# The last half of the output projections: tokens as the outer loop, weight blocks as the inner one

## The chip, the cores and the metric

The kernel runs on one core of a Trainium2 chip. The metric is the device time of one execution in microseconds (us). The core has engines with an instruction queue each: TensorE (PE, matmuls), VectorE (DVE), ScalarE (ACT), GpSimd (POOL), and SyncE (SP), which issues the DMA transfers. They meet only through semaphores.

## The reference

Two layers work on 512 tokens of width 1024. Each adds a gated mixer and a gated mixture of experts to the residual h. This is the part that matters here, cut:

```
for layer in range(2):
    mod = silu(c) @ w_ada[layer] + b_ada[layer]
    sh1, sc1, gt1, sh2, sc2, gt2 = split(mod, 6)
    u = rms_norm(h, norm1) * (1 + sc1) + sh1
    m = mixer_ab(u, ...) if layer == 0 else mixer_c(u, ...)     # both end with  y @ w_out
    h = h + gt1 * m
    u = rms_norm(h, norm2) * (1 + sc2) + sh2
    h = h + gt2 * hier_moe(u, w_grp, b_grp, w_rt, b_rt, w1, w3, w2)
return rms_norm(h, final_norm)
```

`hier_moe` computes 36 logits for each token (4 groups and 32 experts), picks the best group and the two best experts in it, and runs every token through those two (32 experts of 1024 x 512, 512 x 1024 in all).

## The kernel before, in words

All tokens stand on the chip as four tiles t = 0 to 3 of 128 tokens (NT = 4). The program goes through startup, mixer of layer 0, experts of layer 0, mixer of layer 1, experts of layer 1. The weights are streamed from HBM.

**The output projection.** `out_steps` makes `h += gt1 * (y @ w_out)`. It goes over two halves hb = 0, 1 of the 1024 output columns, and over K blocks of 128 rows of `w_out`. A block's half, 128 x 512, is multiplied by the gate (VectorE or GpSimd in turn), and then split (`split`): ScalarE copies it to a rounded part `whi` (L395), and GpSimd subtracts that from it, which gives `wlo` (L396). Both lie in the pool `whl`, which has three buffers of each. `mm3` then makes three matmuls for a tile of tokens: `yhi x whi` (L402), `yhi x wlo` (L403), `ylo x whi` (L404). `steps_rows` makes one step of each block k: its preparation does the gate and the split, and its matmuls go over the four tiles of tokens, so four PSUM banks are open at a time, and all four sums become complete in the last step, three matmuls apart.

When the sum of a tile is complete, `use(t, p)` adds it to h on VectorE (L502). In the last `out_steps` of a layer (K = 4 in layer 0, with `yB`; K = 2 in layer 1, with `yc`) it also calls `done(t, hb)`: that spawns the logits of this half tile, and ScalarE squares the half row of h and sums it (L1309). The logits are four transposes of h on TensorE (L516), a copy to SBUF on VectorE (L1319) or ScalarE (L1321), and, one tick of the stream later, matmuls with the router's weights (L1326). A tick is one `yield` of a step, that is, six matmuls. At the end of all tiles stand the sum of the squares (L1311), a square root on ScalarE (L1312), the reciprocal r (L1313), and on VectorE the logits `lg` from PSUM (L1332), times r (L1333), plus the bias (L1334).

**From there to the experts.** VectorE picks groups and experts in some 25 small instructions, which end with `selb` (L1628). TensorE counts the chosen tokens (L1633, L1634, L1658), VectorE makes places of them (`posm`, L1635) and from those the matrices `Dm` that gather tokens (L1411), TensorE gathers with them (L1426), and the experts' first matmuls (L1502) follow. Meanwhile ScalarE and GpSimd make the normalised h in two parts, `hhi` (L1338) and, for three of the tiles' first halves, `hlo` (L1341, L1342 on GpSimd); VectorE makes the rest (L1347). Two groups of dummy matmuls (`warm`, L178, 20 and 10) stand in TensorE's queue before and after the counting.

**What sets the order.** `run_steps` prepares steps up to two ahead of the one whose matmuls are issued. The order of instructions on each engine is fixed when the program is built: a planner simulates the engines and the pools' buffers, so that a pool with another number of buffers can change the order of all that uses it. The pools `whl` serve all projections of the layer, not only the last.

Of the kernel before, what the change touches and what calls it, by code (L numbers as in the profile page):

```python
# [17 lines left out]
P = 128  # L18
# [3 lines left out]
NT = T // P  # L22
# [67 lines left out]
class Build:  # L90
# [386 lines left out]
    def loader(self, thunks):  # L477
# [3 lines left out]
        def ask(i):  # L481
            if i < len(thunks) and i not in tiles:
                tiles[i] = thunks[i]()
            return tiles.get(i)
# [5 lines left out]
        ask(0)  # L490
        ask(1)

    def out_steps(self, y, K, i0, gate, done=None):


        nc = self.nc
        out = []
        for hb in range(2):
            s = slice(hb * 512, hb * 512 + 512)

            def use(t, p, hb=hb, s=s):
                nc.vector.tensor_add(self.h(t)[:, s], self.h(t)[:, s], p)  # L502
                if done:
                    done(t, hb)

            def ws(k, hb=hb, s=s):
                i = i0 + k // 2
                return self.raw(i)[:, k % 2, s], lambda: self.raw_done(i) if hb and k % 2 else None
            out += self.steps_rows(y, K, ws, use, lambda s=s: gate()[:, s])
        return out  # L510

    def u_transposed(self, hn, h):
# [1269 lines left out]
    def build(self):  # L1782
        tc, nc, a = self.tc, self.nc, self.a
        self.n_ext = 7
        right_side = dict(side="right")
        self.mod, self.ready = {}, set()
        with ExitStack() as es0:
            self.const = self.pool(es0, "const")
            self.gates = self.pool(es0, "gates", 1)
            self.small = self.pool(es0, "small", 2)  # L1790
            self.ring = self.pool(es0, "ring", 2)
            self.psum = self.pool(es0, "psum", 8, space=PSUM)
            self.hroom = self.pool(es0, "hroom", 2)
            self.uroom = self.pool(es0, "uroom", 4)
            self.new_h()
            for l in range(2):
                with ExitStack() as es:
                    self.mix = self.pool(es, "mix%d" % l, 2, **right_side)
                    self.whl = self.pool(es, "whl%d" % l, 3, **right_side)
                    right = self.pool(es, "right%d" % l, 1, **right_side)  # L1800
                    self.stream = st = Stream()
                    with ExitStack() as ms:
                        ut = [self.uroom.tile([P, 4, T], F32R, name="w", tag="w") for _ in range(4)]
                        u = lambda i, k, ut=ut: ut[2 * i + k // 4][:, k % 4]
                        vp = self.pool(ms, "v%d" % l, 2 - l)
                        us = ExitStack()
                        tmp = self.pool(us, "ut%d" % l, 1, **right_side)
                        if l == 0:
                            fin = self.mixer_ab(u, ms, right, *self.startup(u, tmp, us, vp))
                        else:  # L1810
                            fin = self.mixer_c(u, ms, right, self.restart(u, tmp, us, vp))
                        st.until(lambda: not st.q)
                    os_ = ExitStack()
                    self.moe_open(l, os_)
                    self.run_steps(st, fin)
                    st.until(lambda: not st.q)
                self.dump_h("hm%d" % l)
                self.moe(os_)
                if l:
                    self.finish()  # L1820
                os_.close()
                self.dump_h("ho%d" % l)
# [137 lines left out]
```

## Time and profile before

| what | value |
|---|---|
| median of 3 runs | 1747.19 us (1747.1 to 1747.67) |
| the profiled execution's own time | 1746.73 us |
| its span, first to last instruction | 1745.0 us |
| mean granted TensorE clock | 0.973 |
| TensorE busy | 1651.2 us, 95% of the span |
| VectorE, ScalarE, GpSimd busy | 46%, 30%, 23% |
| DMA, mean | 284 GB/s |

How to read it: the profiled execution lies 0.46 us below the median, and 1.73 us of it lie outside the span. TensorE is busy in nearly all of the span; VectorE in less than half of it. The busy shares are means over stages that differ. Times in the rows below are us from the span's start.

### The profile page before, as it was taken

The numbers are of one execution on the slowest core, as the hardware profiler recorded it, in microseconds if no ns is written. First come the engines' busy times: TensorE is split into PE (matmuls) and PEld (weight loads), VectorE is DVE, ScalarE is ACT, GpSimd is POOL, SyncE is SP. The second block draws the span as 40 slices with busy tenths as digits, with TensorE's granted clock in tenths as the row PEclk, the third lists the DMA queues.
The fourth block names the chain that finished last, engine by engine and source line by source line (L and its number), as shares of the span: only waits on it lengthen the run. The fifth ranks groups of instructions, "written<-read, shape, count | busy, mean of one in ns | idle before, by whom it ended". The sixth has DMA issues, their size and how long they took to land. (4 is left out here: it accounts for less than half of the span.)

```text
span 1745.0 us, 23263 instructions
## 1 busy us (share of the span) xinstructions
PE 1651.2 (95%) x9036; PEld 1003.2 (57%) x9036; DVE 806.4 (46%) x1793; ACT 518.9 (30%) x1027; POOL 394.8 (23%) x350
## 2 busy tenths in 40 slices
PE   6999999899999999998988989899999999999996
PEld 3666767544554555454667667678544554555453
DVE  2344653532433233335687787865432433243324
ACT  4745332310110111014636475364310110111013
POOL 2443523210010101001534343353210010101011
PEclk9999999999999999998999999999999999999998
DMA  8655655589999999994243432237599999999992
GB/s 300 223 173 175 217 185 216 221 358 380 413 413 412 413 411 414 411 409 137 63 141 111 132 110 85 85 106 281 226 368 378 413 411 412 413 411 414 412 407 106
DMA packets 156051, 495.89 MB, mean 284 GB/s; under 512 B 16216, under 2 KB 43156, under 8 KB 140576
## 3 DMA queue, kind: packets, MB, share of 16 engines
q1 hardware_dynamic: 155488, 493.23, 73.4%
q8 instruction: 74, 1.21, 0.3%
q10 hardware_dynamic: 448, 1.11, 0.2%
q14 instruction: 41, 0.34, 0.1%
HBM read 492.21 MB, written 2.10 MB: 283 GB/s over the span
## 5 line engine op out<-in xcount | busy, mean ns | idle before, releaser
L1502 PE MATMUL ps<-w,XTm 128*64 128x512 f32 x2048 | 447.2, 593 | 0.0
L1502 PEld LDWEIGHTS ps<-w,XTm 128*64 128x64 f32 x2048 | 161.7, 137 | 267.6 <-issue 260.7
L396 POOL TENSOR_TENSOR wlo<-w,whi 128x512 fp32r<-128x512 f32 x136 | 181.5, 1339 | 269.1 <-ACT whi L395 251.4
L1556 PE MATMUL ps<-w,hT 128*64 128x512 f32 (+1 forms) x1056 | 230.9, 587 | 1.0 <-ACT hT L1534 1.0
L1525 DVE TENSOR_TENSOR gg<-gg,ps 128x512 f32<-128x512 f32 x32 | 22.0, 688 | 377.4 <-PE ps L1502 377.3
L402 PE MATMUL ps<-w,whi 128*128 128x512 f32 x384 | 165.6, 432 | 0.0
L403 PE MATMUL ps<-w,whi 128*128 128x512 f32 x384 | 155.2, 405 | 2.1 <-POOL w L526 1.5
L1556 PEld LDWEIGHTS ps<-w,hT 128*64 128x64 f32 x1056 | 82.2, 137 | 130.2 <-issue 117.5
L404 PE MATMUL ps<-w,wlo 128*128 128x512 f32 x384 | 155.4, 405 | 0.0
L1579 DVE TENSOR_TENSOR w<-w,ps 128x512 f32<-128x512 f32 (+1 forms) x248 | 149.4, 665 | 7.0 <-PE ps L1570 5.5
L1511 POOL CAST sel<-ident 32x128 fp32r<-32x128 f32 x32 | 9.0, 280 | 591.7 <-PE ps L1539 533.9
L1560 POOL TENSOR_TENSOR yl<-y,yh 128x512 fp32r<-128x512 f32 x60 | 76.4, 1274 | 251.3 <-ACT yh L1559 251.3
L1559 ACT ACTIVATE yh<-y 128x512 fp32r<-128x512 f32 (+1 forms) x66 | 40.8, 618 | 295.4 <-DVE y L1558 294.4
L395 ACT ACTIVATE whi<-w 128x512 fp32r<-128x512 f32 x136 | 84.4, 627 | 147.5 <-PE ps L403 81.0
L1426 PE MATMUL ps<-Dm,hhi 128*128 128x256 f32 x512 | 126.2, 288 | 0.0
L1426 PE MATMUL ps<-Dm,hlo 128*128 128x256 f32 x512 | 123.6, 284 | 0.0
L1558 DVE SCALAR_TENSOR_TENSOR y<-ps,wsl,gate 128x512 f32<-128x512 f32 (+1 forms) x66 | 48.5, 735 | 151.5 <-issue 76.3
L1426 PEld LDWEIGHTS ps<-Dm,hhi 128*128 128x128 f32 x512 | 101.5, 199 | 13.4 <-issue 13.3
L1570 PE MATMUL ps<-yh,dt 128*128 128x512 f32 (+1 forms) x264 | 106.0, 406 | 0.0
L1534 ACT ACTIVATE hT<-ps 128x512 f32<-128x512 f32 x32 | 19.1, 598 | 284.2 <-PE ps L1532 265.9
L1426 PEld LDWEIGHTS ps<-Dm,hlo 128*128 128x128 f32 x512 | 101.6, 199 | 0.1
L1570 PE MATMUL ps<-yl,dt 128*128 128x512 f32 (+1 forms) x264 | 100.9, 387 | 0.0
(520 smaller groups left out, 2433.4 us busy)
## 6 DMA issues: line engine op xcount, KB each, us to landing
w<-in_moe_w_dram SPq DMA_DIRECT2D x380, 1024.0 KB, 14.9
w<-in_w_ada_dram SPq DMA_DIRECT2D x40, 1024.0 KB, 5.5
w<-in_w_in_c_dram SPq DMA_DIRECT2D x16, 1024.0 KB, 9.0
w<-in_w_in_ab_dram SPq DMA_DIRECT2D x10, 1024.0 KB
wst<-in_w_ada_dram SPq DMA_DIRECT2D x8, 1024.0 KB, 12.9
w<-in_w_out_ab_dram SPq DMA_DIRECT2D x4, 1024.0 KB, 4.8
w<-in_moe_w_dram SPq DMA_DIRECT2D x8, 512.0 KB, 15.2
w<-in_w_out_c_dram SPq DMA_DIRECT2D x4, 1024.0 KB, 4.9
```

Source lines behind the costliest of these rows:

```text
L395: nc.scalar.activation(hi, src, AF.Copy)
L396: nc.gpsimd.tensor_sub(lo, src, hi.bitcast(F32))
L402: mm(p, lhs[0], rhs[0], start=start, stop=False)
L403: mm(p, lhs[0], rhs[1], start=False, stop=False)
L404: mm(p, lhs[1], rhs[0], start=False, stop=stop)
L1426: nc.tensor.matmul(p, spread(src[:, t], k // 4)[k % 4], Dm[:, t].rearrange("p e s -> p (e s)"), start=t + i == 0, stop=t == NT - 1 and i == 1)
L1502: self.nc.tensor.matmul(ps[j][half[e]], X[:, k, half[e]], w, start=k == 0, stop=k == KD - 1)
L1556: nc.tensor.matmul(py[half[e]], hT[:, k, half[e]], w, start=k == 0, stop=k == 3)
L1558: nc.vector.scalar_tensor_tensor(y32, py, wsl, gate[:, c], op0=OP.mult, op1=OP.mult)
L1560: (nc.vector if last else nc.gpsimd).tensor_sub(yl[:, c], y32, yh[:, c].bitcast(F32))
L1570: mm = nc.tensor.matmul(p, dt[:, t * P:(t + 1) * P], y[:, s], start=i == 0, stop=i == 1)
L1579: nc.vector.tensor_add(h, h, p)
```

## The change

A new `steps_tiles` takes the place of `steps_rows` for the second half (hb = 1) of the last `out_steps` of each layer. It has one step for each tile of tokens; in it, all K blocks of weights are multiplied into one PSUM bank, and `use` follows at once. The preparation of step t does the blocks 2t and 2t + 1, so all blocks stand ready after the second step's preparation, and they are kept until the last tile. For that `whl` gets a fourth buffer in layer 0, where K = 4; in layer 1 it stays at three. The number of instructions on each engine stays the same.

```diff
+    def steps_tiles(self, xs, K, ws, use, scale):
+
+        W = []
+
+        def step(t):
+            def prep():
+                for k in range(2 * t, min(2 * t + 2, K)):
+                    w, after = ws(k)
+                    (self.nc.vector if k % 2 else self.nc.gpsimd).tensor_mul(w, w, scale())
+                    W.append(self.split(w, [P, 512]))
+                    after()
+
+            def mm(_):
+                p = self.ps()
+                for k in range(K):
+                    self.mm3(p, xs(k, t), W[k], k == 0, k == K - 1)
+                    if k % 2:
+                        if k == K - 1:
+                            use(t, p)
+                        yield
+            return prep, mm
+        return [step(t) for t in range(NT)]
...
-            out += self.steps_rows(y, K, ws, use, lambda s=s: gate()[:, s])
+            steps = self.steps_tiles if done and hb else self.steps_rows
+            out += steps(y, K, ws, use, lambda s=s: gate()[:, s])
...
-                    self.whl = self.pool(es, "whl%d" % l, 3, **right_side)
+                    self.whl = self.pool(es, "whl%d" % l, 4 - l, **right_side)
```

In the changed kernel the lines behind the new function have numbers that are 24 higher (the transposes L516 are L540, the logits' matmuls L1326 are L1350).

Three places show what the order of instructions becomes.

TensorE, layer 0, second half, around the end of the first sums. Before, the last block of weights (`whi_2388`) meets the tiles of tokens in turn, and the transposes of the first two tiles (`ps_2426`, `ps_2432`) stand behind the matmuls of the later tiles:

```order
L402 MATMUL ps_2362<-whi_2388,yBhi_1770 128x512 [waits Activation_49]
L403 MATMUL ps_2362<-wlo_2389,yBhi_1770 128x512 [waits Pool_49]
L404 MATMUL ps_2362<-whi_2388,yBlo_1771 128x512
L402 MATMUL ps_2363<-whi_2388,yBhi_1921 128x512
L403 MATMUL ps_2363<-wlo_2389,yBhi_1921 128x512
L404 MATMUL ps_2363<-whi_2388,yBlo_1922 128x512
L402 MATMUL ps_2364<-whi_2388,yBhi_2076 128x512
L516 MATMUL ps_2426<-ident_107,w_76 128x128 [waits DVE_49]
L516 MATMUL ps_2426<-ident_107,w_76 128x128 x3
L403 MATMUL ps_2364<-wlo_2389,yBhi_2076 128x512
```

Now, the first tile's sum (`ps_2367`) ends with its own last block, and its transposes (`ps_2391`) stand directly behind that:

```order
L402 MATMUL ps_2367<-whi_2305,yBhi_1770 128x512
L403 MATMUL ps_2367<-wlo_2306,yBhi_1770 128x512 [waits Pool_49]
L404 MATMUL ps_2367<-whi_2305,yBlo_1771 128x512
L402 MATMUL ps_2367<-whi_2310,yBhi_1770 128x512
L403 MATMUL ps_2367<-wlo_2311,yBhi_1770 128x512 [waits Pool_49]
L404 MATMUL ps_2367<-whi_2310,yBlo_1771 128x512
L540 MATMUL ps_2391<-ident_107,w_76 128x128 [waits DVE_49]
L540 MATMUL ps_2391<-ident_107,w_76 128x128 x3
L402 MATMUL ps_2397<-whi_2283,yBhi_1921 128x512 [waits PE_49]
```

Four matmuls of other tiles stood between a tile's last matmul and its transposes; now there is none. The same holds for the second and the third tile, and the logits' matmuls of tiles 0 to 2 stand in the middle of the next tile's twelve matmuls, where before all four stood behind the last matmul.

TensorE, layer 1, second half, the same place (K = 2, so six matmuls make a tile). Now:

```order
L402 MATMUL ps_9988<-whi_9891,ychi_9519 128x512
L403 MATMUL ps_9988<-wlo_9892,ychi_9519 128x512
L404 MATMUL ps_9988<-whi_9891,yclo_9520 128x512
L1350 MATMUL ps_9997<-wr_6090,scratch_9853 128x36 [waits DVE_49]
L1350 MATMUL ps_9997<-wr_6090,scratch_9853 128x36 x3
L540 MATMUL ps_10002<-ident_107,w_2935 128x128 [waits DVE_49]
L540 MATMUL ps_10002<-ident_107,w_2935 128x128 x3
L402 MATMUL ps_10008<-whi_9886,ychi_9519 128x512 [waits PE_49]
```

Here the logits' matmuls of the tile before (L1350, four instructions that the profile counts as eight) stand between a tile's last matmul and its transposes.

GpSimd, at the startup. The first projection of layer 0 has its low parts of u (`w` from `uf`, L526, now L550) between the splits of the weights. Before:

```order
L396 TENSOR_TENSOR wlo_259<-w_146,whi_258 128x512
L526 TENSOR_TENSOR w_89<-uf_315,w_87 128x512
L396 TENSOR_TENSOR wlo_340<-w_146,whi_339 128x512
L526 TENSOR_TENSOR w_89<-uf_323,w_87 128x512
L396 TENSOR_TENSOR wlo_357<-w_146,whi_356 128x512
```

Now:

```order
L396 TENSOR_TENSOR wlo_259<-w_146,whi_258 128x512
L550 TENSOR_TENSOR w_89<-uf_315,w_87 128x512
L396 TENSOR_TENSOR wlo_340<-w_146,whi_339 128x512
L396 TENSOR_TENSOR wlo_357<-w_146,whi_356 128x512
L550 TENSOR_TENSOR w_89<-uf_323,w_87 128x512
```

With the fourth buffer the fourth split (`wlo_357`) is put ahead of the second low part of u (`w_89<-uf_323`).

## Rows read from the trace of the kernel before

**Rows 1.** Windows, the experts of layer 0: busy us of each engine, clock, DMA share, GB/s

```profile
600.00:620.00 20.00, 20.00 (x97) 10.46 (x93) 5.84 (x13) 2.45 (x4) 2.54 (x2) 1.00 1.02 411
```

**Rows 2.** Windows (PE, PEld, DVE, ACT, POOL, clock, DMA share, GB/s), layer 0's tail

```profile
297.00:308.00 11.00, 11.00 (x55) 9.16 (x55) 2.63 (x5) 2.53 (x6) 1.29 (x1) 1.00 0.28 98
...
323.60:328.40 4.80, 4.79 (x25) 2.22 (x25) 4.16 (x22) 0.00 (x0) 0.00 (x0) 0.50 0.00 0
```

**Rows 3.** Timeline of PE, layer 0: start, duration, what, xcount [idle before, releaser]

```profile
304.85 0.39 PE L404 MATMUL ps<-whi,yBlo 128*128 128x512 f32 x1
...
306.02 0.74 PE L516 MATMUL ps<-ident,w 128*128 128x128 f32 x4
306.52 0.49 PE L403 MATMUL ps<-wlo,yBhi 128*128 128x512 f32 x1
...
308.00 0.39 PE L404 MATMUL ps<-whi,yBlo 128*128 128x512 f32 x1
308.24 1.87 PE L1326 MATMUL ps<-wr,scratch 128*128 128x36 f32 x16
309.94 1.18 PE L516 MATMUL ps<-ident,w 128*128 128x128 f32 x8
...
323.61 0.19 PE L1634 MATMUL ps<-selb,trixb 128*128 128x32 bf16 x1 [4.48 <-DVE selb L1628]
...
332.63 7.09 PE L1502 MATMUL ps<-w,XTm 128*64 128x512 f32 x32
```

**Rows 4.** Timeline of DVE, layer 0

```profile
305.28 1.37 DVE L502 TENSOR_TENSOR w<-w,ps 128x512 f32<-128x512 f32 x2 [7.30 <-PE ps L404]
...
313.86 0.31 DVE L1333 TENSOR_TENSOR lg<-lg,r 128x144 f32<-128x144 f32 x1
...
315.74 1.30 DVE L1605 TENSOR_TENSOR go<-go,gf 128x16 f32<-128x16 f32 x1
...
323.33 0.23 DVE L1628 CAST selb<-self 128x128 bf16<-128x128 f32 x1
```

**Rows 5.** Timeline of ACT, layer 0

```profile
306.00 0.63 ACT L1309 ACTIVATE hhi<-w 128x512 fp32r<-128x512 f32 x1 [6.17 <-DVE w L502]
...
311.21 0.60 ACT L1321 ACTIVATE scratch<-ps 128x512 f32<-128x512 f32 x1 [1.34 <-PE ps L516]
311.83 1.28 ACT L1312 ACT_TABLE_LOAD   x1
```

**Rows 6.** Timeline of PE, layer 1

```profile
1223.38 0.39 PE L404 MATMUL ps<-whi,yclo 128*128 128x512 f32 x1
...
1237.60 0.18 PE L1634 MATMUL ps<-selb,trixb 128*128 128x32 bf16 x1 [3.09 <-DVE selb L1628]
...
1245.39 1.08 PE L1502 MATMUL ps<-w,XTm 128*64 128x512 f32 x4
```

**Rows 7.** Timeline of DVE, layer 1

```profile
1229.15 0.31 DVE L1333 TENSOR_TENSOR lg<-lg,r 128x144 f32<-128x144 f32 x1
...
1237.32 0.23 DVE L1628 CAST selb<-self 128x128 bf16<-128x128 f32 x1
```

**Rows 8.** Timeline of POOL, layer 0's tail

```profile
315.73 1.28 POOL L1342 TENSOR_TENSOR hlo<-hn,hhi 128x512 fp32r<-128x512 f32 x1
```

**Rows 9.** Timeline of POOL, the startup

```profile
34.90 1.26 POOL L526 TENSOR_TENSOR w<-uf,w 128x512 fp32r<-128x512 f32 x1
37.46 1.28 POOL L396 TENSOR_TENSOR wlo<-w,whi 128x512 fp32r<-128x512 f32 x1 [1.30 <-ACT whi L395]
```

**Rows 10.** Timeline of PE, the startup

```profile
36.21 0.50 PE L403 MATMUL ps<-w,whi 128*128 128x512 f32 x1 [1.25 <-POOL w L526]
```

**Rows 11.** Timeline of PE, layer 0's mixer

```profile
102.65 0.50 PE L403 MATMUL ps<-wlo,w 128*128 128x512 f32 x1 [0.50 <-POOL wlo L396]
...
108.94 1.87 PE L265 MATMUL ps<-fold,modrow 128*128 128x1 f32 x8 [3.15 <-DVE modrow L333]
```

**Rows 12.** Timeline of PE, layer 0's mixer, behind a wait of TensorE

```profile
278.80 0.63 PE L404 MATMUL ps<-whi,yBlo 128*128 128x512 f32 x1
```

## The prediction

> **What bounds the kernel now.** I read the summary first, then the windows of the expert stages, then the timelines of the stretches between them. In the experts TensorE is busy 20.00 of 20 us at full clock [rows 1], and it waits for no load there. So a microsecond won or lost ahead of the experts is not made up inside them: it goes through to the end. What counts is when the first expert matmul L1502 starts: 332.63 in layer 0 and 1245.39 in layer 1 [rows 3, 6].
>
> Ahead of it lie two kinds of stretch. In the second half of the last projection, 297 to 308, TensorE is busy 11.00 of 11 us at full clock [rows 2]; it is the bound. Behind its last matmul (308.00 in layer 0, 1223.38 in layer 1 [rows 3, 6]) the chain runs over other engines: add, transposes, copy, square root, then VectorE's routing, `lg` times r at 313.86 and `selb` at 323.33. TensorE then idles 4.48 us for `selb` [rows 3, 4]. In layer 1 the same chain is 1223.38, 1229.15, 1237.32, with 3.09 us of idle [rows 6, 7]. So the edit is judged by two questions: when does the last projection matmul start, and how long is the chain from there.
>
> **The change, layer 0.** Nothing is added or removed; matmuls, adds, squares and copies are as many as before. Two things move the last matmul.
>
> First, the work of the logits that stood behind it comes ahead of it. Sixteen logits matmuls (two tiles) take 308.24 to 309.94, 1.70 us, so 0.85 a tile; the transposes of a tile take 306.02 to 306.52, 0.50 [rows 3]. Tiles 0 and 1's logits matmuls (1.70), tile 2's transposes (0.50) and tile 2's logits matmuls (0.85) are now ahead: 3.05 us. TensorE has no idle time to hide them in [rows 2].
>
> Second, the cover of the adds goes. The way from a tile's last matmul to its transposes is: 304.85 to 305.28, 0.43 until the add starts [rows 3, 4]; one add, 0.69, half of the 1.37 for two [rows 4]; 0.05 until 306.02 [rows 3]. That is 1.17 us, and before it was filled by four matmuls of the next tiles. Now the transposes stand in TensorE's queue directly behind the tile's last matmul, so TensorE stands still for 1.17 less the 0.23 that a matmul takes anyway (308.00 to 308.24 is 0.24 [rows 3]): 0.94 us for each of tiles 0, 1, 2, in all 2.82. All twelve matmuls of the next tile are queued behind that wait. Bounds: 0 if the wait were hidden, 2.82 as worked out; I take the whole, since the same add and the same transposes were timed.
>
> The last matmul then starts at 308.00 + 3.05 + 2.82 = 313.87. What follows it is shorter, as only one tile is left. The add ends 1.12 after it (0.43 + 0.69); the transposes start at 1.17 and, 0.74 long, end at 1.91 [rows 3]. ScalarE has squared by then (0.63 [rows 5]) and copies: from the copy's start at 311.21 to the table load at 311.83 are 0.62, and from the table load to L1333 at 313.86 another 2.03 [rows 4, 5]. With 0.04 until the copy starts L1333 comes 1.95 + 0.62 + 2.03 = 4.60 after the last matmul, against 313.86 - 308.00 = 5.86 before. So it stands at 318.47, **4.6 us later**. The routing behind it keeps its order and its partners on GpSimd, which start with the same r. Bounds: without the stalls +1.8; with the stalls and no shorter chain +5.9.
>
> **Layer 1.** Ahead of the last matmul come 1.70 of logits matmuls and 0.50 of transposes. The logits matmuls of the tile before stand in the gap of the add, so 0.23 + 0.85 of 1.17 are covered, and 0.09 a tile is left, 0.3 in all. The last matmul starts at 1223.38 + 2.5 = 1225.9. There is no table load in this layer's chain, so the last to arrive is the logits' sum: copy done 2.57 behind the last matmul, eight logits matmuls (0.85, and 0.17 until the last result: sixteen are 1.87 long but 1.70 apart [rows 3]), and 0.34 for L1332: 3.9. That gives L1333 at 1229.8, **+0.6** on 1229.15 [rows 7].
>
> Two more terms belong here. The routing from L1333 to `selb` takes 9.47 us in layer 0 and 8.17 in layer 1 [rows 4, 7]. The difference is in VectorE instructions that meet one of GpSimd's L1342: an instruction on 128x16 takes 1.30 us at 315.74, beside an L1342 that starts at 315.73 [rows 4, 8]. The Trainium skill (SBUF — State Buffer, section "Who interferes with whom") says that a VectorE instruction with two SBUF inputs contends with a GpSimd instruction that reads SBUF, and that the loser blocks fully; by that rule the size of the loss depends on the phase alone, and the trace agrees (1.30 us here). In layer 1, r and with it GpSimd move later against the routing, towards the phase of layer 0; I take half of the difference, **+0.65** (bounds 0 and 1.3). From `selb` to L1502 are 9.30 us in layer 0 and 8.07 in layer 1 [rows 3, 4, 6, 7]. In layer 1 three small instructions of the weights stood ahead of `posm`, and in the new order `posm` is first, as in layer 0; the first expert matmuls then wait for the same chain, and TensorE's idle time ahead of it grows from 3.09 towards layer 0's 4.48, after which the dummy matmuls ran at half clock (0.50 [rows 2]). I take layer 0's 9.30, **+1.2** (bounds 0 and 1.2). Layer 1 in all: +2.5, bounds 0.6 and 3.1.
>
> **The fourth buffer.** It changes the order in all of layer 0's mixer. At the startup a split of 1.28 us is put ahead of the low part of u at 34.90 [rows 9], for which TensorE already waits 1.25 us at 36.21 [rows 10]. The wait becomes 2.5: **+1.3** (bounds 0, if something later has slack, and 1.3). Near 108.94 TensorE waits 3.15 us for VectorE [rows 11]; in the new order three projection matmuls that stood ahead of that wait stand behind it. The wait's end is VectorE's, so 3 x 0.23 = **+0.7** come behind it. Bounds: -0.5, if the wait for a low part at 102.65 [rows 11] goes with the buffer, and +1.4, if the three run at the 0.63 us that such a matmul took behind another wait [rows 12] against 0.39 [rows 3]. The loads on SyncE keep their order but for two neighbours, and nothing waits for them here, so they cost nothing; if they did become late, TensorE would show a wait for a load in the first experts.
>
> **Sum.** 4.6 + 2.5 + 1.3 + 0.7 = +9.1 us. The profiled execution took 1746.73 (span 1745.0, 1.73 outside it), 0.46 below the median of the runs, so 1755.8. All bounds together: +1.9 to +11.7, 1748.6 to 1758.4.
>
> **Rivals.**
>
> *Half clock.* The new stalls come three times in a row, in the busiest stretch of the projection. Behind a wait of TensorE the same kind of matmul took 0.63 instead of 0.39 us [rows 12, 3], 0.24 more. If the clock fell in tile 1 and stayed low to the end, 36 matmuls cost 8.6 us more; if it cost one tile only, 2.9. That gives 1758.7 to 1764.4. Against it: stalls of 0.94 between twelve matmuls are much shorter than the wait ahead of 278.80, and the second half ran at 1.00 with the transposes and the logits matmuls in it [rows 2]. The Trainium skill (TensorE: Matmul & The Clock Gate, section "A second HAM failure mode: psum-queue depth-cycling") describes such a case: a kernel that changes PSUM banks with every group idles briefly between the groups, and the clock swings between its two levels. The change does just that; no run here shows it yet.
>
> *Faster.* Were the moved 3.05 us and the stalls free, only the shorter chain would be left: 5.86 to 4.60 in layer 0 (-1.3), 5.77 to 3.9 in layer 1 (-1.9), and -0.5 for the wait at 102.65: 1743.0. It decides once TensorE has some 5.9 us to spare ahead of 308.00 in layer 0. Against it: it is busy 11.00 of 11 us there [rows 2]. Part of it, a shorter chain, is in my sum already.
>
> *Hardly any change.* The stalls are hidden (layer 0 +1.8), layer 1 loses its least (+0.6), and the fourth buffer nothing: 1749.1. For it: an order that is good on one engine can bring slack on another that I don't see. Against it: I know no work that would cover the adds.
>
> **Chances.** What a measurement of this kernel can tell from no change is about 0.2%, 3.5 us: 1743.7 to 1750.7. The forecast with its own range, 1751 to 1758.4, has 0.70. Half clock has 0.10, hardly any change 0.14, faster 0.06. So faster 0.06, within 0.2% 0.14, slower 0.80. The range for 8 in 10 goes from 1748.5 to 1761: it takes in half of the third case and the lower part of the first rival.
>
> **What would show it.** In layer 0's tail: TensorE idle about 0.9 us ahead of the transposes L540 three times, released by VectorE's add; the last L404 near 313.9 plus what came earlier; L1333 some 4.6 behind it; the clock at 1.00. In layer 1: no gap over 0.2 ahead of L540, and L1502 about 9.3 behind `selb`. At the startup a wait of 2.5 us where 1.25 stood. I am wrong if the last matmul is not later by 5 us against the start of the second half, if the routing takes a phase that GpSimd doesn't disturb, or if the startup's wait is taken up by slack behind it.

## The result, and the profile after

The changed kernel takes 1757.2 us (median of 9 runs, 1751.37 to 1761.17), the kernel before 1747.1 (9 runs). The ratio is 1.0054, 95% interval [1.0042, 1.0066]: 7.3 to 11.5 us slower, 9.4 in the middle. The forecast was 1755.8 and +9.1. A second set of runs of the changed kernel (below) gave 1.0057 [1.0044, 1.007].

The profiled execution took 1760.82, which is 14.1 over the profiled execution before and 3.6 over its own median, so its span can't be read against the sum as a whole; I read its places one by one. The first view is the timeline of TensorE in layer 0, the second half (columns: start, duration, engine, line, operation, count, idle before and what ended it):

```profile
300.17 0.48 PE L402 MATMUL ps<-whi,yBhi 128*128 128x512 f32 x1
...
304.57 0.40 PE L404 MATMUL ps<-whi,yBlo 128*128 128x512 f32 x1
305.75 0.74 PE L540 MATMUL ps<-ident,w 128*128 128x128 f32 x4 [0.78 <-DVE w L525]
...
310.95 0.74 PE L540 MATMUL ps<-ident,w 128*128 128x128 f32 x4 [0.78 <-DVE w L525]
...
316.15 0.74 PE L540 MATMUL ps<-ident,w 128*128 128x128 f32 x4 [0.78 <-DVE w L525]
...
320.17 0.40 PE L404 MATMUL ps<-whi,yBlo 128*128 128x512 f32 x1
321.35 0.74 PE L540 MATMUL ps<-ident,w 128*128 128x128 f32 x4 [0.78 <-DVE w L525]
...
334.34 0.19 PE L1658 MATMUL ps<-selb,trixb 128*128 128x32 bf16 x1 [5.13 <-DVE selb L1652]
```

The same places on VectorE:

```profile
324.64 0.31 DVE L1357 TENSOR_TENSOR lg<-lg,r 128x144 f32<-128x144 f32 x1
...
334.06 0.23 DVE L1652 CAST selb<-self 128x128 bf16<-128x128 f32 x1
```

Where [rows 3] have the transposes of the first two tiles inside the matmuls of later tiles, TensorE now waits for VectorE's add ahead of each tile's transposes. From 304.57 to 305.75 are 1.18 us, 0.95 more than a matmul takes, three times as forecast (the fourth stands behind the last matmul). Of these 0.95 the view shows 0.78 as idle, since the matmul's own duration overlaps it. The last matmul to L1357 is 320.17 to 324.64, 4.47 us (forecast 4.60, before 5.86), and L1357 to `selb` 9.42 (before 9.47).

The second half starts with the first line above, at 300.17. In the kernel before it starts here:

```profile
294.31 0.48 PE L402 MATMUL ps<-whi,yBhi 128*128 128x512 f32 x1
```

Counted from there, the last matmul stands at 20.00 us instead of 13.69, 6.3 later (forecast 3.05 + 2.82 = 5.87), and L1357 at 24.47 instead of 19.55, 4.9 later (forecast 4.6).

The windows over that stretch and over the dummy matmuls behind `selb` (busy us of PE, PEld, DVE, ACT, POOL, then granted clock, DMA share, GB/s):

```profile
307.00:320.50 13.50, 11.94 (x66) 9.49 (x64) 2.35 (x4) 2.05 (x5) 0.00 (x0) 1.00 0.01 2
334.30:339.00 4.70, 4.66 (x25) 2.05 (x25) 4.03 (x22) 0.00 (x0) 0.00 (x0) 0.50 0.00 0
```

In spite of the waits the granted clock stayed at 1.00. TensorE was busy 11.94 of 13.50 us, where [rows 2] show 11.00 of 11.

Layer 1, TensorE:

```profile
1239.40 0.39 PE L404 MATMUL ps<-whi,yclo 128*128 128x512 f32 x1
1239.63 0.97 PE L1350 MATMUL ps<-wr,scratch 128*128 128x36 f32 x8
1240.57 0.75 PE L540 MATMUL ps<-ident,w 128*128 128x128 f32 x4
...
1252.42 0.19 PE L1658 MATMUL ps<-selb,trixb 128*128 128x32 bf16 x1 [3.99 <-DVE selb L1652]
...
1252.80 4.43 PE L178 MATMUL ps<-onesb 128*128 128x512 bf16 x10
...
1261.29 7.09 PE L1526 MATMUL ps<-w,XTm 128*64 128x512 f32 x32
...
1283.14 7.09 PE L1580 MATMUL ps<-w,hT 128*64 128x512 f32 x32 [0.26 <-ACT hT L1558]
```

and VectorE:

```profile
1243.52 0.31 DVE L1357 TENSOR_TENSOR lg<-lg,r 128x144 f32<-128x144 f32 x1
...
1252.14 0.23 DVE L1652 CAST selb<-self 128x128 bf16<-128x128 f32 x1
```

The logits' matmuls fill the add's time, and no wait is left ahead of L540. L1357 comes 4.12 us behind the last matmul (forecast 3.9), `selb` 8.62 later (8.17 before [rows 7], 8.8 forecast), and the first expert matmul 9.15 behind `selb` (8.07 before [rows 6, 7], 9.3 forecast). But look at the last line of TensorE, the second group of matmuls of the first expert, 7.09 us long. These are the rows of the kernel before there:

```profile
1237.97 3.65 PE L178 MATMUL ps<-onesb 128*128 128x512 bf16 x10
...
1267.25 8.78 PE L1556 MATMUL ps<-w,hT 128*64 128x512 f32 x32 [0.26 <-ACT hT L1534]
```

The same 32 matmuls took 8.78 us. The changed kernel pays 0.78 more for its ten dummy matmuls (4.43 against 3.65) and gets 1.69 back in the first expert.

The startup, TensorE after, where [rows 10] show 1.25:

```profile
37.48 0.50 PE L403 MATMUL ps<-w,whi 128*128 128x512 f32 x1 [2.48 <-POOL w L550]
```

### The profile page after: what moved, and what is told of

It is laid out like the page before. It is cut to its first block, busy times and chain, and to the rows that moved or that the text cites. A ratio compares the mean times of both kernels' runs of the same rounds, so it can differ in the third digit from the quotient of the medians.

```text
span 1759.1 us, 23257 instructions
## 1 busy us (share of the span) xinstructions
PE 1659.6 (94%) x9036; PEld 1008.2 (57%) x9036; DVE 805.6 (46%) x1793; ACT 518.3 (29%) x1027; POOL 394.3 (22%) x350
```

## The experiments

My theory: three independent costs, the order in layer 0 (+4.6), the order in layer 1 (+2.5), the fourth buffer (+2.0). The rivals differ in where the 9 us lie. Ratios are to the kernel before, run on the same chip, with the 95% interval; 0.001 is 1.75 us.

**The change again**, for a second profile:

> The changed kernel once more, for a second profile. If the costs are in the order of the instructions, the same places cost the same again: TensorE waits 0.95 us ahead of each tile's transposes in layer 0 and 2.5 us at the startup, and the median is some 9 to 10 us over the kernel before (about 1756). If the stretches at half clock ahead of the last projection belong to the order too, they stand at the same places with the same number of matmuls. Rival: they fall anew in every execution, then their sum differs by some us from the first profile (11.0 us more time not at full clock than in the kernel before) while the waits stay.

1756.99 us, 1.0057 [1.0044, 1.007]. The three waits and the startup's 2.48 us are there again. Matmul for matmul the two profiles stay within 0.3 us of each other until 998 us; between 999 and 1006 the first loses 2.5 us in the mixer of layer 1, with matmuls of 0.63 us, that the second doesn't lose (granted clock 0.86 over 985 to 1010 in the first, 1.00 in the second). So one stretch at half clock in layer 1 doesn't come with the program. That those ahead of the last projection do is not shown by these two alone: the kernel before and two runs below (layer 1 alone, and 14 dummy matmuls) have the same order of instructions on every engine up to the experts of layer 0, and their profiles still differ there. Against the kernel before, the run with layer 1 alone is 0.7 us ahead at 257 us, 2.3 ahead at the first expert matmul of layer 0, and 0.7 ahead again at 360 us.

**The fourth buffer alone** (`3` to `4 - l` in the pool `whl`, nothing else):

> Only the fourth buffer in layer 0; both halves of the projection keep weights as the outer loop. By my terms the startup's wait goes from 1.25 to 2.5 us (+1.3) and the displaced matmuls near 109 cost 0.7: +2.0, about 1749. Rival 1, from the first profile after the change, where the first expert stage was already some 6 us late at the start of the second half: the fourth buffer carries about +6, 1753. Rival 2, slack behind the startup takes it up: within 1 us of the kernel before.

1752.61, 1.0032 [1.002, 1.0044]: +5.6. My +2.0 was too small, and rival 1 right. At the startup this profile loses 2.8 us, 1.2 by the longer wait and the rest by eight matmuls at half clock behind it (the two profiles of the changed kernel lose 1.2). Behind the startup, the place where it loses most of what I had not priced is 208 to 235 (times of the kernel before). VectorE there works out the scale of a head's rows in small instructions on 128x4, and multiplies the rows by it (`orow`):

```profile
217.31 1.22 DVE L377 TENSOR_SCALAR or<-rsx 128x4 int32<-128x4 int32 x1
218.56 1.19 DVE L379 SCALAR_TENSOR_TENSOR rsz<-or 128x4 f32<-128x4 f32 x1
219.79 1.19 DVE L380 TENSOR_TENSOR rsz<-rsz,rsx 128x4 f32<-128x4 f32 x1
...
222.39 1.13 DVE L877 TENSOR_SCALAR orow<-ps,or 128x128 f32<-128x128 f32 x4
```

GpSimd and TensorE beside it:

```profile
215.95 5.00 POOL L396 TENSOR_TENSOR wlo<-w,whi 128x512 fp32r<-128x512 f32 x4
```

```profile
223.31 0.80 PE L402 MATMUL ps<-whi,yAhi 128*128 128x512 f32 x1 [0.71 <-DVE orow L877]
223.90 0.63 PE L403 MATMUL ps<-wlo,yAhi 128*128 128x512 f32 x1
224.33 0.63 PE L404 MATMUL ps<-whi,yAlo 128*128 128x512 f32 x1
```

and VectorE, GpSimd and TensorE in the kernel before:

```profile
215.25 0.17 DVE L377 TENSOR_SCALAR or<-rsx 128x4 int32<-128x4 int32 x1
215.46 0.16 DVE L379 SCALAR_TENSOR_TENSOR rsz<-or 128x4 f32<-128x4 f32 x1
...
218.29 1.12 DVE L877 TENSOR_SCALAR orow<-ps,or 128x128 f32<-128x128 f32 x4
```

```profile
212.21 2.98 POOL L396 TENSOR_TENSOR wlo<-w,whi 128x512 fp32r<-128x512 f32 x2
216.58 1.26 POOL L396 TENSOR_TENSOR wlo<-w,whi 128x512 fp32r<-128x512 f32 x1 [1.39 <-ACT whi L395]
```

```profile
220.50 0.63 PE L402 MATMUL ps<-whi,yAhi 128*128 128x512 f32 x1
```

The extra buffer lets four splits run in a row on GpSimd, where the kernel before has a gap behind two of them, and the three instructions on 128x4 stand in that gap. Beside the splits they take 1.2 us instead of 0.16; the time is in the instructions themselves, and the view shows no wait ahead of them. `orow` is late, TensorE waits for it, and behind that wait its matmuls run at 0.63 us. From 208.9 to 234.9 the program falls back by 2.1 us against the kernel before, in this profile and in both of the changed kernel. About 1.0 of that is the wait, counted by the starts of the matmuls. The rest is half clock, and the kernel before has some there too, without a wait ahead of it (the last line above is one of four such matmuls; with four buffers there are six; granted clock 0.76 over 218 to 222 before, 0.71 over 220 to 226 with four buffers). That the wait makes this stretch longer is read from the profiles, not tested.

**The same without the startup** (the extra buffer is a pool of its own, used for every fourth split behind the first eight):

```diff
-        hi = self.whl.tile(shape, F32R, name="whi", tag="whi")
+        pool = self.whx if self.whx and n >= 8 and n % 4 == 3 else self.whl
+        hi = pool.tile(shape, F32R, name="whi", tag="whi")
```

> Weights as the outer loop everywhere; the fourth buffer comes into use only behind the startup, so that the startup keeps its order and all that follows has the order of the kernel with four buffers. If the fourth buffer's cost of 5.6 us is a sum of places, the startup's part goes (1.2 to 2.8 in three profiles) and 3 to 4.5 are left: about 1750. Rival: the startup's wait is the whole cause, and what follows only shifts with it: within 1 us of the kernel before. Rival 2: the startup's part is taken up later, and all of 5.6 stays.

1750.38, 1.0026 [1.0017, 1.0035]: +4.5. The startup's part is about 1, and most lies behind it. Two more runs split the rest (`8 <= n < 40` and `n >= 40` in that line):

> Weights as the outer loop everywhere; a fourth buffer for splits only between the startup and about 200 us, so that of the moves it makes only the one near 109 is left (three matmuls behind the wait for modrow instead of ahead of it). My term for it was 0.7, bounds -0.5 and 1.4: about 1747. Rival: this place carries most of the 4 us that the fourth buffer costs behind the startup: 1750.

> The complement: a fourth buffer for splits only from about 200 us on. From the profiles, the gate products and splits that it lets run ahead at 211 to 222 delay the chain of small VectorE instructions to the rows of the gated heads there (three of them take 1.2 us instead of 0.16), TensorE waits for these, and the clock falls longer: 2.1 us in four profiles, less 0.8 near 257. So +1.5 to +3: about 1749. Rival: nothing here, the place near 109 is all: within 1 us of the kernel before.

The early part gave 1746.53, 0.9998 [0.9989, 1.0007], the later one 1748.03, 1.0004 [0.9995, 1.0014]. Their profiles fit the place: the later one falls back by 2.2 us from 208.9 to 234.9, the early one by nothing. In the timed runs, however, the two together make +0.4 and not 4.5, though the upper ends of their intervals (1.2 and 2.4) together reach over the lower end of the other (3.0). The later run's eleven times lie in two groups, five from 1745.1 to 1746.5 and six from 1748.0 to 1751.1, and its profile (1749.24) is of the second group, so the 2.2 us need not be lost in every execution. How the 4.5 us are shared out stays open.

**Tokens outside in layer 0 alone**, with a buffer of its own for the fourth block, so that the startup and the rest keep three:

```diff
-                    W.append(self.split(w, [P, 512]))
+                    W.append(self.split(w, [P, 512], self.whx if k == 3 else None))
```

> Tokens as the outer loop in layer 0 alone, and the fourth block of weights in a buffer of its own, so that the pool keeps three buffers and the startup its order. By my terms +4.6 (3.05 of logits work moved ahead, 2.82 of uncovered adds, a chain shorter by 1.26): about 1751.5; L1333's successor (lg times r) 4.6 us behind the last matmul of the projection. Rival, the stalls also drop the clock: the second half shows matmuls at 0.63 us and +7 or more. Rival, the change in layer 0 is free once the order ahead of it stays: within 1 us.

1749.1, 1.0019 [1.0011, 1.0028]: +3.3, interval 1.9 to 4.9. My 4.6 is in it. The waits are the same 0.78 of idle. In the profile, `lg` times r is late by the same 4.9 us, counted from the start of the second half, but a part comes back in the first expert. These are its second group of matmuls in layer 0 in this run, in the run with layer 1 alone (whose layer 0 has the order of the kernel before), and in the kernel before:

```profile
356.91 7.09 PE L1581 MATMUL ps<-w,hT 128*64 128x512 f32 x32 [0.26 <-ACT hT L1559]
```

```profile
352.18 8.64 PE L1580 MATMUL ps<-w,hT 128*64 128x512 f32 x32 [0.26 <-ACT hT L1558]
```

```profile
354.49 7.09 PE L1556 MATMUL ps<-w,hT 128*64 128x512 f32 x32 [0.26 <-ACT hT L1534]
```

The granted clock is 1.00 over 356.9 to 364 in this run and 0.82 over 352.2 to 361 in the one with layer 1 alone. At the start of the group this run is 4.73 us behind the one with layer 1 alone, at its end 3.18, near the +3.3 of the timed runs. The profile of the kernel before is the exception: of the eight profiles with weights outside in layer 0 it alone has 7.09, and the other seven have 8.64 to 8.78. Against the run with layer 1 alone it had lost 1.4 us before, between 265 and 280 us.

**The same with the transposes six matmuls later**:

```diff
-            self.stream.spawn(logits(t, hb), 1)
+            self.stream.spawn(logits(t, hb), 2 if hb and not l else 1)
```

> As the run with tokens outside in layer 0 alone and a buffer of its own for the fourth block, but the transposes of a tile are put six matmuls later, behind the middle of the next tile. By my terms the three waits of 0.95 go, and the third tile's logits matmuls stand behind the last matmul again: the last matmul 2.2 later than before instead of 5.9, lg times r 4.6 behind it, so 0.9 over the kernel before, and 3.4 under the run without the delay. Rival: the waits were not the cause, and moving the transposes leaves the time at +3.

1745.67, 0.9998 [0.9989, 1.0007]. The waits are gone from its timeline of TensorE:

```profile
298.49 0.40 PE L405 MATMUL ps<-whi,yBlo 128*128 128x512 f32 x1
298.72 0.63 PE L541 MATMUL ps<-ident,w 128*128 128x128 f32 x4
299.11 0.48 PE L403 MATMUL ps<-whi,yBhi 128*128 128x512 f32 x1
...
308.59 0.39 PE L405 MATMUL ps<-whi,yBlo 128*128 128x512 f32 x1
308.82 0.97 PE L1351 MATMUL ps<-wr,scratch 128*128 128x36 f32 x8
309.76 0.74 PE L541 MATMUL ps<-ident,w 128*128 128x128 f32 x4
```

3.4 us less than the run before it by the medians, as the term said. One number decides where the transposes and the logits' matmuls of a tile stand, the work is the same, and the loss goes. Both profiles have the 7.09 us in the first expert of layer 0, so it isn't that exchange. The delay does two things at once, by my terms: it covers the three waits (2.8 us), and it puts the logits' matmuls of the third tile behind the last matmul again (0.85).

**Layer 1 alone** (`K == 2` added to the condition, three buffers):

> Tokens as the outer loop in layer 1 alone, three buffers in both layers. By my terms +2.5: about 1749.5, of which 0.6 until lg times r, 0.65 in the routing, 1.2 from selb to the first expert matmul. Rival, from the first profile after the change: the first expert matmul is 2.3 later, but the first experts give 1.7 back, as the eight matmuls at half clock that the kernel before shows there do not come: +0.5, no difference that can be told.

1746.69, 1.0002 [0.9993, 1.0011]: +0.3, so the rival was right. Its profile shows both sides of the exchange:

```profile
1237.80 0.19 PE L1658 MATMUL ps<-selb,trixb 128*128 128x32 bf16 x1 [4.01 <-DVE selb L1652]
...
1238.17 4.43 PE L178 MATMUL ps<-onesb 128*128 128x512 bf16 x10
...
1268.38 7.09 PE L1580 MATMUL ps<-w,hT 128*64 128x512 f32 x32 [0.26 <-ACT hT L1558]
```

Against the kernel before, it falls back by 2.2 us between the last transposes of the mixer's rows (1199.1) and the first expert matmul, and gains 1.7 in the first expert. I thought that the longer idle time (4.01 instead of 3.09) decides. **A run to test that**: the kernel before with 14 dummy matmuls instead of 20 ahead of `selb` in layer 1.

> The kernel before, with 14 instead of 20 dummy matmuls ahead of selb in layer 1, so that TensorE idles some 4.4 us there instead of 3.1, as it does in layer 0 and with the changed kernel. If the longer idle time decides where the clock falls, the ten dummy matmuls behind it run at half clock throughout (4.43 us instead of 3.65), the first expert matmul is some 1 us later against selb, and the matmuls at half clock in the first expert (1.7 us) go: within 1 us of the kernel before, with the loss moved. Rival: the first expert's half clock stays, then +1.

1746.87, 1.0001 [0.9992, 1.001], and the mechanism fails:

```profile
1237.02 0.18 PE L1634 MATMUL ps<-selb,trixb 128*128 128x32 bf16 x1 [4.38 <-DVE selb L1628]
...
1237.40 3.54 PE L178 MATMUL ps<-onesb 128*128 128x512 bf16 x10
...
1266.55 8.78 PE L1556 MATMUL ps<-w,hT 128*64 128x512 f32 x32 [0.26 <-ACT hT L1534]
```

With 4.38 us of idle the dummy matmuls were as fast as with 3.09, and the first expert as slow. The length of the idle time doesn't decide; what does stays open.

**Both layers, without the two costs that can be taken away:**

> Tokens outside in both layers, with the buffer of its own and the later transposes in layer 0: the change without the two costs that can be taken from it. If the parts add up, 0.9 from layer 0 and 0.3 to 0.5 from layer 1, about 1747.5, no difference from the kernel before. Rival: the loop order itself costs 3 us or more, whatever covers the adds.

1746.48, 1.0000 [0.9991, 1.0009]. The loop order itself costs nothing that can be told.

**A try for a faster version**: the low part of u for which TensorE waits at the startup goes to VectorE, on top of the delayed transposes and on the kernel before (`k % 2 and (l or k != 3)` chooses the engine).

> The run with the later transposes and the buffer of its own, and at the startup the fourth low part of u on VectorE, which is idle there from 34.4 us on, instead of GpSimd behind a split. TensorE's wait of 1.25 us goes: 1.2 less than that run, about 1745, and faster than both kernels if it holds. Rival: later waits take it up, no difference from the kernel before.

> The kernel before with that low part on VectorE alone: 1.2 to 1.4 less than before, about 1745. If it gains as much as the run with the later transposes and the same low part, the gain has nothing to do with the loop order.

1745.93, 0.9995 [0.9986, 1.0004], and 1746.64, 1.0001 [0.9992, 1.001]. No gain that can be told. In the second profile the wait shrank from 1.25 to 0.58 only:

```profile
34.74 0.51 PE L403 MATMUL ps<-w,whi 128*128 128x512 f32 x1 [0.58 <-DVE w L526]
```

No version here is faster than the kernel before by more than the runs can tell.

## Why the prediction was right, and where it was not

The sum was right: +9.1 forecast, +9.4 and +10.0 measured. The parts add up too: 5.6 (fourth buffer) + 3.3 (layer 0) + 0.3 (layer 1) = 9.2. But two of my three terms were mis-sized, one down and one up, and that the sum came out is luck: 3.6 us too little for the buffer stand against 1.3 and 2.2 too much for the two layers.

- **Layer 0, +4.6 forecast, +3.3 (1.9 to 4.9) measured.** The mechanism is shown: three waits of 0.95, a chain of 4.47, L1357 4.9 us later, and the loss gone when the transposes stand later. The estimate lies in the interval; the profiles put the difference of 1.6 into the first expert, as in the next point.
- **Layer 1, +2.5 forecast, +0.3 (-1.2 to 1.9) measured.** Each step came nearly as forecast (L1357, routing, `selb` to the first expert matmul). The step that failed is the first one of the whole argument: "a microsecond won or lost ahead of the experts is not made up inside them". It was read from a window in the middle of the experts [rows 1], and the first expert is not like it. In layer 1, 1.7 us come back there, since the matmuls at half clock of the kernel before don't occur. In layer 0 the step seems to hold, as the distance between the two first profiles stays at 10.54 us from the first expert matmul to 800 us (times of the kernel before). But that rests on one profile of the kernel before; against the other seven with weights outside, 1.6 to 1.7 us come back there too.
- **The fourth buffer, +2.0 forecast, +5.6 (3.5 to 7.7) measured.** At the startup the wait became 2.48 as worked out (+1.2). The three displaced matmuls near 109 were a small term, as said (+0.7, measured with the early run -0.3, interval -1.9 to 1.2). What was missing, as far as the profiles tell, is a place that I had not priced, since I looked for moved matmuls on TensorE: GpSimd's splits moved too, and beside four of them in a row VectorE's chain was late, 2.1 us in the profiles. The timed run for it gave +0.7 (-0.9 to 2.4). The parts timed apart (1.1 for the startup, -0.3, +0.7) make 1.5 of the 5.6, so most of that cost has no place that is shown. The rows for this kind of loss stood in my own text, for the routing [rows 4, 8]; I didn't ask where else the moved splits would meet VectorE.
- **Half clock in the second half of the projection** did not come: 1.00 over 307 to 320.5. The Trainium skill's case of groups in changing PSUM banks with short idle times between them (TensorE: Matmul & The Clock Gate, "A second HAM failure mode: psum-queue depth-cycling") is not what this trace shows, with 0.78 us of idle behind every twelve matmuls. This rival's price was read too high as well: it took the durations, 0.63 against 0.39, but matmuls overlap. Their starts lie 0.43 apart at half clock (223.90 and 224.33) and 0.23 at full clock, so one costs 0.20 more and not 0.24.
- **The faster rival** was wrong for the reason given: with the waits gone and most of the logits' work still moved the time is that of before, not below it.

## What to carry to other kernels

When a loop is turned so that a sum is finished earlier, look at what stood between its last matmul and its first consumer in the queue: that work was the cover of an add on another engine, and with it gone the wait is paid once per tile. Here, delaying the consumer by six matmuls gave back all that the runs can tell. And a pool with one more buffer is a change of order for everything that uses the pool; price each engine's moved instructions where they meet the other engines, not only TensorE's.

## What the runs showed that I had not expected

The half clock behind `selb` comes in two forms. In the 14 profiles there are 28 such stretches. In 10 of them the ten dummy matmuls run at half clock to the end (first to last 3.79 us) and the first expert's second group of 32 takes 7.09 us; in the other 18 the dummy matmuls are faster (1.94 to 3.42) and that group takes about 8.7. No stretch has ten slow dummy matmuls and a slow group, and none has neither. So a delay ahead of it can be given back, and a gain can be lost, without any change in the work. In layer 1 the first form came in all four profiles with tokens outside, the second in all ten with weights outside. In layer 0 the first form came in five of six with tokens outside and in one of eight with weights outside, the kernel before. As the same order of instructions gave both forms there, the order alone doesn't decide; what does stays open.
